# How the row-shifted copies of the value tile are made, in the input projection of a hybrid decoder layer

## The chip, the cores and the metric

One core of one Trainium2 chip runs the whole layer. The metric is the device time of one execution in microseconds (us); the kernel before takes 1537.65 us, the median of three runs that lie between 1537.08 and 1538.68.

## What is computed

The reference is one decoder layer over 256 rows of 2048 features, in float32, batch 1. Cut to what matters here:

```python
h = rmsnorm(x, norm_mix_w)
proj = h @ w_in                                   # q, k, v, z, b, a, pool, g_a, g_b
q, k, v, ... = split(proj)
qkv = silu(causal_dwconv(concat(q, k, v), conv_qkv_w))     # CONV_QKV = 4 taps
q = l2norm(q) * HEAD_DIM ** -0.5 ; k = l2norm(k)           # 16 heads of 128
o = gated_delta_rule(q, k, v, g_log, beta)        # 4 chunks of 64 rows
y_a = rmsnorm(o, gdn_norm_w) * silu(z)
y_b = (causal_multiscale_pool(p_in) @ pool_w) * pool_scale
x = x + (sigmoid(g_a) * y_a + sigmoid(g_b) * y_b) @ w_out
x = x + (gelu(causal_dwconv(gate) + b) * up) @ w_down      # ffn, then a last rmsnorm
```

The depthwise convolution takes, for each feature, row i times tap 3, plus row i-1 times tap 2, row i-2 times tap 1 and row i-3 times tap 0; rows above the first are zero. A kernel that holds rows on partitions must therefore bring rows i-1, i-2 and i-3 to the partition of row i.

## The kernel before

Every large product is made from float32 weights that are split in two halves of fewer bits. A weight tile of 512 KB (128 partitions by 2 by 512) arrives by SyncE's queue (SP) as `raw` (L223, four buffers). ScalarE (ACT) casts it to `whi` (L317), VectorE (DVE) subtracts `raw - whi` to give `wlo` (L328), and TensorE (PE) does twelve 128x512 matmuls on each tile: L365 (`whi` with the high half of the rows), L366 (`whi` with the low half) and L367 (`wlo` with the high half), four of each. `gemm_a` runs eight such tiles for one 256x512 block of the projection. Up to two tiles beyond the current one are asked for ahead (AHEAD = 2); `whi` and `wlo` have three buffers. SP's instructions run in order, so a `raw` load that waits for its buffer, or any other transfer that waits, holds all transfers behind it.

The mixing stage, up to about 770 us, loops over g = 0..3 (four heads each). For each g it makes the blocks K, Q, V, P (pool), the gates and Z. A finished block is taken out of PSUM by `evict`: ACT scales it into the tile `ev` (L781, tag `ev`, a single buffer).

- K and Q are turned so that features lie on partitions, and convolved by `conv_silu`: ACT makes tap 3, DVE adds the three others as twelve instructions of about 254 columns (L839), ACT takes the tanh (L844), and DVE writes `kq` (L846). The working tile has tag `cy`, two buffers. Later DVE takes sums of squares of the heads (L906, from PE's small products at L901).
- V keeps its rows on partitions. `ev` is written by SP to the DRAM scratch `vrow` (L1122), behind three rows of zeros that ACT's queue has put there at the start (L774, from the tile `zr` that DVE clears at L771). Then `v_moved` multiplies `ev` by tap 3 into `vt` (DVE, L802) and reads three copies `mv` back from `vrow`, shifted by j = 1, 2, 3 rows (SP, L807). Copies 1 and 2 are in the two `cy` buffers, which they share with `conv_silu`; copy 3 has the buffer of tag `mv`. `v_conv` does for j = 1, 2, 3: `mv *= tap` (L816) and `vt += mv` (L817), then a tanh on ACT and one more product (L822).
- `gdn` then goes on with the heads: decays, `ga` (L920), small tables sent out to DRAM as `cdd` (L939) and brought back to many partitions as `lb`, the triangular inverse (L965, L967), and the state recurrence.

What stands where on each engine is decided at build time by a scheduler that places instructions by its own estimate of when they are ready, apart from places that `issue_after` ties to an earlier instruction (in `v_conv`, each tap follows a certain `wlo`). So the conv's instructions, the `wlo` subtractions and the sums of squares stand mixed on DVE in one fixed order, and the transfers of the conv and of the weights in one fixed order on SP.

Of the kernel before, what the change touches and what calls it, by code (L numbers as in the profile page):

```python
# [8 lines left out]
F32 = mybir.dt.float32  # L9
# [5 lines left out]
P = 128  # L15
S = 256
# [19 lines left out]
def kernel(  # L36
# [20 lines left out]
    nc = tc.nc  # L57
# [5 lines left out]
    dpool = ctx.enter_context(tc.tile_pool(name="dram", bufs=2, space=bass.MemoryType.DRAM))  # L63
# [5 lines left out]
    def nm(s):  # L69
        cnt[0] += 1  # L70
        return f"{s}_{cnt[0]}"
# [282 lines left out]
    def gemm_a(lh, ll, nk, steps=None, ps=None):  # L354

        ps = pm() if ps is None else ps
        for c in range(nk // 2) if steps is None else steps:
            if c == 1:
                while later:
                    later.pop(0)()  # L360
            hi, lo = weights()
            for kk in range(2):
                k = 2 * c + kk
                for t in range(2):
                    mm(ps[:, t, :], lh(k, t), hi[:, kk, :], start=(k == 0), stop=False)  # L365
                    mm(ps[:, t, :], ll(k, t), hi[:, kk, :], start=False, stop=False)  # L366
                    mm(ps[:, t, :], lh(k, t), lo[:, kk, :], start=False, stop=(k == nk - 1))  # L367
                side()
        return ps
# [65 lines left out]
    mp = mix.__enter__()  # L435
# [46 lines left out]
    def parts_x(pts):  # L482
        for k, pt in pts:
            high, low = (both(xhl, k)[:, n, :] for n in range(2))
            hi = nc.scalar.activation(high, pt, AF.Copy, scale=nmw[:, k : k + 1])
            lo = nc.vector.scalar_tensor_tensor(low, pt, nmw[:, k : k + 1], high.bitcast(F32),
                                                op0=ALU.mult, op1=ALU.subtract)
        return hi.ins, lo.ins
# [28 lines left out]
    with tc.manual_schedule(engines={mybir.EngineType.PE, mybir.EngineType.DVE, mybir.EngineType.Activation}):  # L517
# [21 lines left out]
        for c in range(4):  # L539
            if c:  # L540
                tile_k0(2 * c)
            if c < 3:
# [3 lines left out]
                last_act, last_dve = parts_x(pts[2:])  # L546
# [219 lines left out]


    SH = 3
    vrow = dpool.tile([4, SH + S, 512], F32, tag="vrow", bufs=1, name="vrow")
    zr = mp.tile([P, 2, 512], F32, tag="mv", name="zr")  # L770
    nc.vector.memset(zr[:SH, 0, :], 0.0)  # L771
    for g in range(4):
        with tc.issue_after(last_act):
            nc.scalar.dma_start(vrow[g, 0:SH, :], zr[:SH, 0, :])  # L774

    def evict(ps, by=None):

        by = rs1 if by is None else by
        e = mp.tile([P, 2, 512], F32, tag="ev", bufs=1, name=nm("ev"))
        for t in range(2):  # L780
            nc.scalar.activation(e[:, t, :], ps[:, t, :], AF.Copy, scale=by[:, t : t + 1])  # L781
        return e
# [17 lines left out]
    def v_moved(e, g, vt):  # L800

        nc.vector.tensor_tensor(vt, e, taps_of[g][3], op=ALU.mult)  # L802
        moved_of[g] = []
        splits_of[g] = len(splits)
        for j in (1, 2, 3):
            m = mp.tile([P, 2, 512], F32, name=nm("mv"), **(dict(tag="cy", bufs=2) if j < 3 else dict(tag="mv")))
            nc.sync.dma_start(m, vrow[g, SH - j : SH - j + S, :].rearrange("(t p) d -> p t d", p=P))  # L807
            moved_of[g].append(m)

    def v_conv(g, vt):  # L810
# [284 lines left out]
    for g in range(4):  # L1095
        kq = mp.tile([P, 4, 2, S], F32, tag="kq", bufs=1, name=nm("kq"))
        for kind, dst in ((1, kq[:, :, 0, :]), (0, kq[:, :, 1, :])):
            ps = ps_k0 if kind == 1 and g == 0 else gemm_a(xh, xl, KD)
            e = evict(ps)
# [19 lines left out]

            later.append(after_k)  # L1120
        e = evict(gemm_a(xh, xl, KD), rsh)
        nc.sync.dma_start(vrow[g, SH : SH + S, :].rearrange("(t p) d -> p t d", p=P), e)  # L1122
        later.append(lambda e=e, g=g, vt2=vt2: v_moved(e, g, vt2))


# [3 lines left out]
        e = evict(ps) if g == 3 else evict(ps, rsh)  # L1129
# [608 lines left out]
```

## Time and profile before

| what | value |
|---|---|
| median of three runs | 1537.65 us |
| the profiled execution's own time | 1538.56 us |
| its span in the profile | 1536.8 us |
| granted TensorE clock, mean | 0.998 |
| TensorE matmul busy | 1524.3 us, 99% of the span |
| VectorE busy | 1268.3 us, 83% |
| ScalarE busy | 853.1 us, 56% |
| GpSimd busy | 80.9 us, 5% |
| SyncE's queue, share of 16 DMA engines | 59.2% |

A row of a group names the line of the kernel, the engine, the operation, then what is written and what is read, the shape, and the time of it; in a timeline the start comes first, and a bracket at the end of a row tells how long the engine had been idle and what ended that. A matmul of 128x512 shows as 0.39 us though the next one starts 0.227 us after it, because matmuls overlap: a stall of TensorE shows as idle time only where it is longer than that overlap of 0.16 us. A row of waits tells who waited, for whom, how long in all, how many times, and the longest.

### The profile page before, as it was taken

Reading aid. Unit: us, or ns where it says so; the run is one execution under the profiler, and the core shown is the slowest. Engines: PE = TensorE matmul, PEld = TensorE weight load, DVE = VectorE, ACT = ScalarE, POOL = GpSimd, SP = SyncE. Lnnn points to the kernel's source line nnn. Section 1 sums busy time; section 2 is a strip of 40 time slices with the busy share of each in tenths; the row PEclk is TensorE's granted clock in tenths of the full one; section 3 lists DMA queues with packets and bytes.
Section 4 is the critical chain, followed back from the end, with each engine's and each line's share of the span. In section 5 each row is a group of like instructions: output and inputs, shape, how many; then the busy total and the mean of one; then the engine's idle time right before and its main releaser. Section 6 shows DMA issues by size and latency. Waiting matters only on the chain. (4 is left out here: it accounts for less than half of the span.)

```text
span 1536.8 us, 20233 instructions
## 1 busy us (share of the span) xinstructions
PE 1524.3 (99%) x7290; PEld 1255.4 (82%) x7290; DVE 1268.3 (83%) x1793; ACT 853.1 (56%) x1070; POOL 80.9 (5%) x105
## 2 busy tenths in 40 slices
PE   9999999999999999999999999999999999999997
PEld 8887888787878888788888888788888888888876
DVE  6788859896589858887567899999999886889896
ACT  6455446454455445454455666666666665555553
POOL 1010002000100000000000000000000011010200
PEclk9999999999999999999999999999999999999999
DMA  8776757776576766776588556656457478566662
GB/s 276 209 229 198 203 165 207 218 216 185 148 250 201 208 169 194 231 195 186 171 263 305 179 178 219 219 206 206 154 165 243 127 238 266 172 223 207 235 201 98
DMA packets 166515, 313.62 MB, mean 204 GB/s; under 512 B 19554, under 2 KB 23426, under 8 KB 166286
## 3 DMA queue, kind: packets, MB, share of 16 engines
q1 hardware_dynamic: 157280, 283.17, 59.2%
q0 software_dynamic: 7344, 27.27, 5.5%
q10 hardware_dynamic: 1790, 1.89, 0.4%
q8 instruction: 57, 0.93, 0.3%
q14 instruction: 44, 0.36, 0.1%
HBM read 303.33 MB, written 8.95 MB: 203 GB/s over the span
## 5 line engine op out<-in xcount | busy, mean ns | idle before, releaser
L317 ACT CAST whi<-raw 128x1024 fp32r<-128x1024 f32 x420 | 441.2, 1052 | 427.1 <-PE psm L366 270.0
L328 DVE TENSOR_TENSOR wlo<-raw,whi 128x1024 fp32r<-128x1024 f32 x418 | 507.7, 1220 | 146.0 <-ACT whi L317 140.2
L317 ACT CAST whi<-quad 128x1024 fp32r<-128x1024 f32 x182 | 190.5, 1053 | 136.8 <-PE psg L1418 43.5
L328 DVE TENSOR_TENSOR wlo<-quad,whi 128x1024 fp32r<-128x1024 f32 x182 | 220.0, 1219 | 30.0 <-ACT whi L317 29.4
L367 PE MATMUL psm<-wlo,xhl 128*128 128x512 f32 x432 | 169.5, 393 | 1.3 <-DVE wlo L328 1.2
L365 PE MATMUL psm<-whi,xhl 128*128 128x512 f32 x432 | 169.0, 391 | 0.0
L366 PE MATMUL psm<-whi,xhl 128*128 128x512 f32 x432 | 168.6, 390 | 0.0
L1418 PE MATMUL psg<-whi,fhl 128*128 128x512 f32 x504 | 127.2, 390 | 0.0
L1418 PEld LDWEIGHTS psg<-whi,fhl 128*128 128x128 f32 x504 | 94.5, 188 | 19.6
L367 PEld LDWEIGHTS psm<-wlo,xhl 128*128 128x128 f32 x432 | 81.1, 188 | 18.8 <-DVE wlo L328 2.2
L366 PEld LDWEIGHTS psm<-whi,xhl 128*128 128x128 f32 x432 | 81.1, 188 | 16.8
L365 PEld LDWEIGHTS psm<-whi,xhl 128*128 128x128 f32 x432 | 81.1, 188 | 16.7
L244 DVE TENSOR_TENSOR quad<-quad,quad 128x1024 f32<-128x1024 f32 x72 | 87.6, 1216 | 0.0
L1418 PE MATMUL psg<-wlo,fhl 128*128 128x512 f32 x252 | 69.9, 389 | 0.0
L1418 PE MATMUL psg<-whi,ups 128*128 128x512 f32 x216 | 58.9, 394 | 0.0
L1418 PEld LDWEIGHTS psg<-wlo,fhl 128*128 128x128 f32 x252 | 47.3, 188 | 9.9
L1403 PE MATMUL psm<-whi,hhi 128*128 128x512 f32 (+1 forms) x140 | 54.5, 389 | 0.1
L1403 PE MATMUL psm<-whi,hlo 128*128 128x512 f32 (+1 forms) x140 | 54.1, 386 | 0.0
L1403 PE MATMUL psm<-wlo,hhi 128*128 128x512 f32 (+1 forms) x140 | 54.0, 387 | 0.0
L365 PE MATMUL psm<-whi,mhi 128*128 128x512 f32 x128 | 50.8, 397 | 0.0
L367 PE MATMUL psm<-wlo,mhi 128*128 128x512 f32 x128 | 50.0, 390 | 0.0
L366 PE MATMUL psm<-whi,mlo 128*128 128x512 f32 x128 | 49.9, 390 | 0.0
(435 smaller groups left out, 2953.7 us busy)
## 6 DMA issues: line engine op xcount, KB each, us to landing
raw<-in_w_in_dram SPq DMA_DIRECT2D x224, 512.0 KB, 4.3
raw<-in_w_up_dram SPq DMA_DIRECT2D x104, 512.0 KB, 4.8
quad<-in_w_up_dram SPq DMA_DIRECT2D x72, 512.0 KB, 5.0
raw<-in_w_down_dram SPq DMA_DIRECT2D x56, 512.0 KB, 5.1
raw<-in_w_out_dram SPq DMA_DIRECT2D x32, 512.0 KB, 4.2
quad<-in_w_down_dram POOLq DMA_DIRECT2D x32, 512.0 KB, 5.3
mv<-vrow SPq DMA_DIRECT2D x12, 512.0 KB, 4.8
taps<-in_conv_qkv_w_dram SPq DMA_DIRECT2D x16, 256.0 KB, 6.6
```

Of the source, the lines that this page charges most:

```text
L244: nc.vector.tensor_tensor(out_, plus_, minus_, op=ALU.subtract)
L317: last_cast[0] = nc.scalar.copy(hi, raw).ins
L328: last_split[0] = nc.vector.tensor_tensor(lo, raw, hi.bitcast(F32), op=ALU.subtract).ins
L365: mm(ps[:, t, :], lh(k, t), hi[:, kk, :], start=(k == 0), stop=False)
L366: mm(ps[:, t, :], ll(k, t), hi[:, kk, :], start=False, stop=False)
L367: mm(ps[:, t, :], lh(k, t), lo[:, kk, :], start=False, stop=(k == nk - 1))
L1403: mm(ps[:, cs], lhs(kk), part_[:, kk, cs], start=(first and kk == 0 and n == 0), stop=(last and kk == 1 and n == 2), skip_group_check=shared)
L1418: mm(ps, lhs(kk), w[n][:, kk], start=(first and n == 0 and kk == 0 and lhs is high), stop=False, skip_group_check=True)
```

## The change

The scratch `vrow`, the zeros `zr` and their four transfers go. For each shift j the copy is now made inside the chip: GpSimd (POOL) clears the first j rows of the first half of `mv` (L801 of the changed kernel), and SP issues three transfers from `ev` to `mv`: 112 partitions moved by j (L802), the remaining 16 - j partitions (L803), and the last j partitions of the first half to the first j partitions of the second half (L804). Copy 1 is now in the buffer of tag `mv`, and copies 2 and 3 are in the `cy` buffers. The convolution's own arithmetic is the same. Line numbers of the changed kernel are 6 lower at `evict`, 3 lower from the convolution to the eviction of V, and 4 lower behind it.

```diff
     SH = 3
-    vrow = dpool.tile([4, SH + S, 512], F32, tag="vrow", bufs=1, name="vrow")
-    zr = mp.tile([P, 2, 512], F32, tag="mv", name="zr")
-    nc.vector.memset(zr[:SH, 0, :], 0.0)
-    for g in range(4):
-        with tc.issue_after(last_act):
-            nc.scalar.dma_start(vrow[g, 0:SH, :], zr[:SH, 0, :])
...
         for j in (1, 2, 3):
-            m = mp.tile([P, 2, 512], F32, name=nm("mv"), **(dict(tag="cy", bufs=2) if j < 3 else dict(tag="mv")))
-            nc.sync.dma_start(m, vrow[g, SH - j : SH - j + S, :].rearrange("(t p) d -> p t d", p=P))
+            m = mp.tile([P, 2, 512], F32, name=nm("mv"), **(dict(tag="cy", bufs=2) if j > 1 else dict(tag="mv")))
+            nc.gpsimd.memset(m[0:j, 0, :], 0.0)
+            nc.sync.dma_start(m[j : 112 + j], e[:112])
+            nc.sync.dma_start(m[112 + j :], e[112 : P - j])
+            nc.sync.dma_start(m[0:j, 1, :], e[P - j :, 0, :])
             moved_of[g].append(m)
...
         e = evict(gemm_a(xh, xl, KD), rsh)
-        nc.sync.dma_start(vrow[g, SH : SH + S, :].rearrange("(t p) d -> p t d", p=P), e)
         later.append(lambda e=e, g=g, vt2=vt2: v_moved(e, g, vt2))
```

The scheduler places the instructions anew. All four groups and all engines differ only up to the end of the mixing stage; behind it the orders are the same. Three places follow.

SP, in group 2, from the eviction of V on: before, one write to `vrow`, one weight tile, and the three reads of 512 KB.

```order
L1122 DMA vrow<-ev_4083 128x2x512
L223 DMA raw_4172<-in_w_in_dram 128x2x512
L807 DMA mv_4112<-vrow 128x2x512
L807 DMA mv_4114<-vrow 128x2x512
L807 DMA mv_4116<-vrow 128x2x512
L223 DMA raw_4190<-in_w_in_dram 128x2x512
```

After, in the same place (`mv_4120`, `mv_4125`, `mv_4130` are the copies 1, 2 and 3):

```order
L804 DMA mv_4120<-ev_4092 1x16x32
L802 DMA mv_4120<-ev_4092 112x1024
L803 DMA mv_4120<-ev_4092 15x1024
L802 DMA mv_4125<-ev_4092 112x1024
L803 DMA mv_4125<-ev_4092 14x1024
L804 DMA mv_4125<-ev_4092 2x512
L223 DMA raw_4189<-in_w_in_dram 128x2x512
L223 DMA raw_4207<-in_w_in_dram 128x2x512
L223 DMA raw_4225<-in_w_in_dram 128x2x512
L802 DMA mv_4130<-ev_4092 112x1024
L803 DMA mv_4130<-ev_4092 13x1024
L804 DMA mv_4130<-ev_4092 3x512
```

Five transfers became twelve, the copies stand where the write to DRAM stood, and the third copy stands three weight tiles further back.

DVE, in group 2, before: the convolution of V, the `wlo` of the next weight tiles and the sums of squares (L906).

```order
L816 TENSOR_TENSOR mv_4112<-mv_4112,taps_3817 128x1024
L328 TENSOR_TENSOR wlo_4158<-raw_4154,whi_4156 128x1024
L817 TENSOR_TENSOR vt_3813<-vt_3813,mv_4112 128x1024
L816 TENSOR_TENSOR mv_4114<-mv_4114,taps_3814 128x1024
L906 ISA jk_3946,ssk_3883<-psg_3942,ident 128x128
...
L816 TENSOR_TENSOR mv_4116<-mv_4116,taps_3814 128x1024
L817 TENSOR_TENSOR vt_3813<-vt_3813,mv_4114 128x1024
L906 ISA jk_3946,ssk_3883<-psg_3944,ident 128x128
...
L328 TENSOR_TENSOR wlo_4176<-raw_4172,whi_4174 128x1024
L817 TENSOR_TENSOR vt_3813<-vt_3813,mv_4116 128x1024
```

After (L813 and L814 are the lines L816 and L817 of before, L843 is L846, L903 is L906):

```order
L813 TENSOR_TENSOR mv_4120<-mv_4120,taps_3826 128x1024
L328 TENSOR_TENSOR wlo_4157<-raw_4153,whi_4155 128x1024
L813 TENSOR_TENSOR mv_4125<-mv_4125,taps_3823 128x1024
L843 SCALAR_TENSOR_TENSOR kq_3481<-th_3875,cy_3858 128x4x256
L814 TENSOR_TENSOR vt_3822<-vt_3822,mv_4120 128x1024
L328 TENSOR_TENSOR wlo_4175<-raw_4171,whi_4173 128x1024
L328 TENSOR_TENSOR wlo_4193<-raw_4189,whi_4191 128x1024
L814 TENSOR_TENSOR vt_3822<-vt_3822,mv_4125 128x1024
L813 TENSOR_TENSOR mv_4130<-mv_4130,taps_3823 128x1024
L328 TENSOR_TENSOR wlo_4211<-raw_4207,whi_4209 128x1024
L903 ISA jk_3955,ssk_3892<-psg_3951,ident 128x128
...
L814 TENSOR_TENSOR vt_3822<-vt_3822,mv_4130 128x1024
```

Between the first product of the conv and its last sum there stood two `wlo`; there now stand four and the `kq` of Q, and the first sum of squares comes two `wlo` later.

DVE, in group 3, before: from the `wlo` ahead of the conv to the `wlo` in the middle of it.

```order
L802 TENSOR_TENSOR vt_5350<-ev_5620,taps_5354 128x1024
L846 SCALAR_TENSOR_TENSOR kq_5009<-th_5403,cy_5386 128x4x256
L328 TENSOR_TENSOR wlo_5659<-raw_5655,whi_5657 128x1024
L328 TENSOR_TENSOR wlo_5677<-raw_5673,whi_5675 128x1024
L816 TENSOR_TENSOR mv_5649<-mv_5649,taps_5354 128x1024
L328 TENSOR_TENSOR wlo_5695<-raw_5691,whi_5693 128x1024
L817 TENSOR_TENSOR vt_5350<-vt_5350,mv_5649 128x1024
```

After (L796 is the product with tap 3, L836 the taps of Q's own convolution):

```order
L796 TENSOR_TENSOR vt_5367<-ev_5637,taps_5371 128x1024
...
L328 TENSOR_TENSOR wlo_5684<-raw_5680,whi_5682 128x1024
L836 SCALAR_TENSOR_TENSOR cy_5403<-psg_5393,cqw,cy_5403 128x254
L813 TENSOR_TENSOR mv_5665<-mv_5665,taps_5371 128x1024
L836 SCALAR_TENSOR_TENSOR cy_5403<-psg_5398,cqw,cy_5403 128x254
L328 TENSOR_TENSOR wlo_5702<-raw_5698,whi_5700 128x1024
L813 TENSOR_TENSOR mv_5670<-mv_5670,taps_5368 128x1024
L836 SCALAR_TENSOR_TENSOR cy_5403<-psg_5393,cqw,cy_5403 128x253
L814 TENSOR_TENSOR vt_5367<-vt_5367,mv_5665 128x1024
L836 SCALAR_TENSOR_TENSOR cy_5403<-psg_5398,cqw,cy_5403 128x253
L328 TENSOR_TENSOR wlo_5720<-raw_5716,whi_5718 128x1024
```

Two `wlo` stood between tap 3 and the first product on a copy; one stands there now, and Q's own convolution, which was over before tap 3, now lies between the steps of V's.

## Prediction

> **What bounds the kernel now.** I read the page's busy line first, then what PE waits for, then the stretches of the mixing stage.
>
> ```profile
> span 1536.8 us, 20233 instructions
> PE 1524.3 (99%) x7290; PEld 1255.4 (82%) x7290; DVE 1268.3 (83%) x1793; ACT 853.1 (56%) x1070; POOL 80.9 (5%) x105
> PE psm L367 <- DVE wlo L328: 1.5, 2, 1.2
> DVE mv L816 <- DMA mv<-vrow: 11.2, 4, 4.5
> ACT whi L317 <- DVE mv L816: 4.3, 1, 4.3
> ```
>
> TensorE is busy 99% of the span, and the change touches none of its matmuls. So nothing is won but where PE stands still, and nothing is lost but where PE is made to stand still. DVE waits 11.2 us for the row-shifted copies, four times, which looks like the prize; but PE waits for DVE's `wlo` only 1.5 us. What carries over from DVE to PE is read from the stretches (us, then PE, PEld and DVE busy):
>
> ```profile
> 140.00:160.00 20.00, 19.69 (x85) 15.53 (x86) 19.36 (x36) 12.13 (x19) 0.00 (x0) 1.00 0.74 210
> 280.00:300.00 20.00, 19.86 (x84) 15.47 (x83) 19.46 (x37) 8.54 (x9) 2.76 (x2) 1.00 0.58 170
> 440.00:460.00 20.00, 19.75 (x84) 15.37 (x82) 14.95 (x19) 9.20 (x10) 0.00 (x0) 1.00 0.80 267
> 460.00:480.00 20.00, 19.05 (x85) 15.22 (x85) 19.43 (x41) 7.88 (x10) 3.09 (x2) 1.00 0.56 163
> ```
>
> These are the stretches near the four convolutions where PE falls short of 20: 0.31 + 0.14 + 0.25 + 0.95 = 1.65 us. Group 3 has none. In three of the four DVE is at 97%, so a delay there goes straight into `wlo`. The idle time hides 0.16 us of each stall (a matmul shows 0.39 us, the next starts 0.227 us after it), so I count from start to start. The largest stall, in group 2, with the DVE rows that make it:
>
> ```profile
> 452.43 1.23 DVE L816 TENSOR_TENSOR mv<-mv,taps 128x1024 f32<-128x1024 f32 x1 [4.48 <-DMA mv<-vrow]
> 459.67 1.22 DVE L328 TENSOR_TENSOR wlo<-raw,whi 128x1024 fp32r<-128x1024 f32 x1
> 459.36 0.39 PE L366 MATMUL psm<-whi,xhl 128*128 128x512 f32 x1
> 460.95 0.50 PE L367 MATMUL psm<-wlo,xhl 128*128 128x512 f32 x1 [1.20 <-DVE wlo L328]
> 461.28 0.39 PE L365 MATMUL psm<-whi,xhl 128*128 128x512 f32 x1
> ```
>
> DVE stood 4.48 us until 452.43, worked without a gap, and began the `wlo` that PE needed at 459.59 only at 459.67. PE lost 460.95 - 459.36 - 0.23 = 1.36 us, and the matmul after it came 0.10 us late (0.33 instead of 0.23): 1.46 us. Groups 0 and 1:
>
> ```profile
> 99.69 1.23 DVE L816 TENSOR_TENSOR mv<-mv,taps 128x1024 f32<-128x1024 f32 x1 [2.25 <-DMA mv<-vrow]
> 137.35 0.42 DVE L965 TENSOR_TENSOR tmp<-lb,tb 128x248 f32<-128x248 f32 x1 [3.08 <-DMA lb<-cdd]
> 139.86 0.50 PE L367 MATMUL psm<-wlo,xhl1a 128*128 128x512 f32 x1
> 140.20 0.40 PE L365 MATMUL psm<-whi,xhl1a 128*128 128x512 f32 x1
> 148.25 0.39 PE L366 MATMUL psm<-whi,xhl2b 128*128 128x512 f32 x1
> 148.95 0.50 PE L367 MATMUL psm<-wlo,xhl2b 128*128 128x512 f32 x1 [0.31 <-DVE wlo L328]
> 275.97 1.23 DVE L816 TENSOR_TENSOR mv<-mv,taps 128x1024 f32<-128x1024 f32 x1 [2.29 <-DMA mv<-vrow]
> 281.54 0.39 PE L366 MATMUL psm<-whi,xhl 128*128 128x512 f32 x1
> 282.07 0.50 PE L367 MATMUL psm<-wlo,xhl 128*128 128x512 f32 x1
> ```
>
> Group 0 loses 148.95 - 148.25 - 0.23 = 0.47 and 0.11 behind it, and 0.11 at each of three restarts from 140.20 (0.34 instead of 0.23): 0.9 us. Group 1 loses 0.30 + 0.1 = 0.4. In all **2.8 us** is within the change's reach.
>
> **The change, part by part.** The path to the first product now goes from `ev` to `mv` by one transfer, not two:
>
> ```profile
> 442.40 0.37 SPq L1122 DMA_DIRECT2D vrow<-ev  x1
> 448.50 1.39 SPq L807 DMA_DIRECT2D mv<-vrow  x3
> 620.97 0.37 SPq L1122 DMA_DIRECT2D vrow<-ev  x1
> 624.73 1.39 SPq L807 DMA_DIRECT2D mv<-vrow  x3
> mv<-vrow SPq DMA_DIRECT2D x12, 512.0 KB, 4.8
> vrow<-ev SPq DMA_DIRECT2D x4, 512.0 KB, 4.9
> whole<-y POOLq DMA_DIRECT2D x3, 512.0 KB, 3.8
> xtd<-xt POOLq DMA_DIRECT2D x4, 512.0 KB, 6.1
> TT<-tbd SPq DMA_DIRECT2D x16, 32.0 KB, 2.2
> x<-in_x_dram SPq DMA_DIRECT2D x3, 512.0 KB, 8.6
> raw<-in_w_in_dram SPq DMA_DIRECT2D x224, 512.0 KB, 4.3
> L317 ACT CAST whi<-raw 128x1024 fp32r<-128x1024 f32 x420 | 441.2, 1052 | 427.1 <-PE psm L366 270.0
> L328 DVE TENSOR_TENSOR wlo<-raw,whi 128x1024 fp32r<-128x1024 f32 x418 | 507.7, 1220 | 146.0 <-ACT whi L317 140.2
> ```
>
> The reads waited 6.1 us (group 2) and 3.8 us (group 3) for the write to land. That goes. No row shows a copy from SBUF to SBUF. Its bounds: not under the 2.2 us of a small transfer, not over the 8.6 us of the slowest 512 KB one; I take 4.3 to 4.8, as the reads of the same size by the same queue. The rests of 13 to 15 rows (up to 60 KB) and the single rows (2 to 6 KB) I bound by 2.2 and 4.8, so they land with the large piece issued just ahead. On SP three issues at 1.39 / 3 = 0.46 us replace one: nine instead of four, 2.3 us more per group, which pushes later `raw` tiles back by up to 2.8 us. Cover: `raw` loads run about four tiles ahead (4 x 2.72 = 10.9 us, against 4.3 for landing, 1.05 for `whi`, 1.22 for `wlo`); about 4 us remains, and beyond it each us would cost one.
>
> [...]
>
> The POOL clears cost at most the 0.77 us of POOL's mean instruction (80.9 / 105), on an engine busy 5%. Copies 2 and 3 are in `cy`, so the third clear waits for Q's `kq` to release its buffer; behind it on SP stand weight loads and on POOL small work for the heads, whose readers come after the convolution. In group 2 that puts the third copy's landing near 458, and DVE comes to its product about then. Removing the early clear and four small transfers changes nothing: at that time PE is fed by other work.
>
> Group by group, with copy 1 issued where the write was issued:
> - **Group 0.** Copy 1 lands about 93 to 94, before DVE asks at 97.4 (99.69 less 2.25). The 2.25 us go. DVE is then full to 134 and sends its decay table earlier by as much; the 3.08 us wait for `lb` shrinks to about 0.9 and the 0.9 us of PE stalls, which lie in a saturated stretch just behind it, should go. Gain 0.9 (nothing, if the table's own transfers set it).
> - **Group 1.** Copy 1 lands about 271 instead of 275.97. DVE's order changes, its work does not; the `wlo` in question ends 2 us before PE asks. Gain 0.4.
> - **Group 2.** Copy 1 lands at about 447.5, so 4.48 us of waiting shrink to little. In its place stand the later `kq` and the wait for copy 3; adding 1.14 us per 128x1024 step in the new order leaves each `wlo` 0.9 to 1.5 us ahead of PE. Gain 1.46.
> - **Group 3.** Here is no stall to win, and the new order is tighter:
>
> ```profile
> 620.98 1.23 DVE L802 TENSOR_TENSOR vt<-ev,taps 128x1024 f32<-128x1024 f32 x1
> 628.71 1.22 DVE L816 TENSOR_TENSOR mv<-mv,taps 128x1024 f32<-128x1024 f32 x1 [2.22 <-DMA mv<-vrow]
> 624.61 0.39 PE L367 MATMUL psm<-wlo,xhl1a 128*128 128x512 f32 x1
> ```
>
> PE begins the low half of a tile at 624.61; three tiles on, with the heads' small products now behind them, it needs `wlo` at 624.61 + 3 x 2.72 = 632.77. From copy 1's landing DVE does two conv products and a sum (3 x 1.14), three taps of Q (0.4 each) and two `wlo` (1.14 + 1.22) ahead of it: 6.9 us. So the landing may be 625.9 at the latest. Issued at 621.4, at 4.3 to 4.8 us it lands at 625.7 to 626.2: a stall of 0 to 0.3, and I charge 0.3.
>
> **The sum**: 2.8 - 0.3 = 2.5 us off the profiled execution's 1538.56: 1536.1. That execution was 0.9 above the median of the runs, so against the median 1537.65: **1535.2 us**, 0.16% less. This kernel's measurement tells about 0.2% (3.1 us) from no change, so most of this forecast lies within it.
>
> **The rivals.**
> - **Only the plain stalls go.** Group 0's chain over `lb` stays, or group 2's stall is replaced by one behind `kq` and copy 3. Then 0.4 + 1.46 - 0.3, or 0.9 + 0.4 - 0.3: 1536.1 to 1536.7. For it: the new DVE order holds four `wlo` and a `kq` in the same stretch. Still no measurable change.
> - **The copies land late, and the kernel is slower.** Place: group 3, where DVE's wait for copy 1 stands ahead of two `wlo`. The price is one us per us beyond 625.9. At 6.1 us (`xtd`) that is 1.6 there, and about half of group 2's and group 1's gain is lost: about 1538. At 8.6 us it is 4.1; groups 1 and 2 then get copy 1 at 276 and 451, as before, and gain nothing: 1537.65 + 4.1 - 0.5 = 1541. It decides from about 8 us. Against it: every 512 KB row by SP inside the kernel lies at 4 to 5 us.
> - **SP is blocked.** The third copy waits for `kq`, and `raw` loads stand behind it; if the 4 us cover is gone in one or two groups by 2 us each, the time is 1535.2 + 2 to 4, about 1538.
> - **More goes than I see.** DVE gains 11 us of slack in all, and if it also removes restarts of 0.1 to 0.2 us at other tiles (some ten), 1 us more: 1534.2.
> - **The change doesn't remove the wait**, because DVE's new place for the product comes as late as before: about 1537.7.
>
> **How the numbers follow.** Forecast (both groups of stalls gone, 1534.6 to 1536) 0.42; only the plain stalls 0.15; SP blocked, small delay or no effect 0.13; more than I see 0.16; slower by late copies 0.14. Faster by over 0.2% is under 1534.6: the fourth case and some of the spread of the first, 0.22. Slower is over 1540.7: 0.14. Within: 0.64. The range takes the first four cases and the late copies up to 8.6 us: 1533.9 to 1541.0.
>
> **What would show it.** Right: no wait of DVE for `mv` over 2 us in groups 0 to 2; copy 1 lands within 5 us of its issue; PE full at 460:480 but for a few tenths; PE's wait at `wlo` near 633 at most 0.3 us. Wrong: landing times over 6 us, PE idle in 620:660, ACT's `whi` waiting for `raw` behind the copies, or a new wait of DVE for the third copy's `mv` that ends later than 460.

## The result, and the profile after

The changed kernel takes 1541.9 us, the median of 14 runs (1539.79 to 1547.43); the kernel before, run beside it, 1537.53 (1534.92 to 1539.68). The ratio is 1.0031, 95% interval 1.0022 to 1.0039: **4.4 us slower**, where 2.5 us faster was forecast and 1533.9 to 1541.0 was the range.

The page of the changed kernel, and what its PE and DVE wait for (us in total, times, the longest):

```profile
span 1540.7 us, 20299 instructions
PE 1524.2 (99%) x7290; PEld 1254.7 (81%) x7290; DVE 1266.7 (82%) x1792; ACT 852.5 (55%) x1070; POOL 83.6 (5%) x117
PE psm L367 <- DVE wlo L328: 4.5, 5, 1.5
PE psg L1008 <- DVE T L984: 1.4, 2, 0.7
DVE mv L813 <- DMA mv<-ev: 9.7, 5, 4.0
DVE tmp L962 <- DMA lb<-cdd: 13.5, 4, 5.5
```

PE's work is the same; its wait for `wlo` went from 1.5 to 4.5 us, and a wait for `T` (the inverse that the heads of group 3 need) is new. DVE's wait for the shifted copies hardly fell, 11.2 to 9.7. Its wait for `lb`, the decay table that returns from DRAM, is 13.5 us; before it was 5.2 in total. The stretches (us, PE busy second):

```profile
280.00:300.00 20.00, 19.03 (x81) 14.77 (x80) 19.14 (x41) 8.60 (x10) 2.01 (x2) 1.00 0.60 164
460.00:480.00 20.00, 20.00 (x86) 15.90 (x85) 18.00 (x43) 9.11 (x10) 2.02 (x2) 1.00 0.57 162
480.00:500.00 20.00, 19.19 (x89) 15.57 (x88) 14.61 (x19) 10.31 (x15) 0.00 (x0) 1.00 0.68 183
660.00:680.00 20.00, 18.53 (x88) 14.95 (x86) 14.06 (x21) 8.52 (x11) 0.00 (x0) 1.00 0.69 188
680.00:700.00 20.00, 19.04 (x84) 15.44 (x84) 19.39 (x38) 10.22 (x17) 0.00 (x0) 1.00 0.77 206
720.00:740.00 20.00, 18.57 (x160) 14.60 (x160) 14.09 (x26) 8.29 (x13) 0.00 (x0) 1.00 0.51 161
```

The old stall of group 2 at 460 is gone, as forecast. Group 1's has grown, a new one stands near 497, and three stand in group 3, behind the convolution: 1.47 + 0.96 + 1.43 = 3.9 us, about the whole difference of the two spans (1540.7 against 1536.8); in groups 1 and 2 the visible idle time is 0.83 more, 1.20 less and 0.81 more, which nearly cancels. The chain that ends in these three stalls is seen on POOL, SP, DVE and PE. First the end of the sums of squares (`nk` on POOL follows the last of them) and the decay table of group 3 before:

```profile
649.55 1.01 POOL L911 TENSOR_TENSOR nk<-ssk,half 128x4 f32<-128x4 f32 x1 [7.25 <-DVE ssk L910]
652.66 3.65 SPq L939 DMA_DIRECT2D cdd<-ga  x8
657.56 1.74 SPq L942 DMA_DIRECT2D lb<-cdd  x4
```

and the same of the changed kernel, with what comes ahead of the sums and what DVE and PE do behind the table:

```profile
635.20 0.52 POOL L801 MEMSET mv<- 3x512 f32 x1 [14.24 <-DVE vt L814]
641.70 1.23 DVE L813 TENSOR_TENSOR mv<-mv,taps 128x1024 f32<-128x1024 f32 x1 [3.20 <-DMA mv<-ev]
654.93 1.01 POOL L908 TENSOR_TENSOR nk<-ssk,half 128x4 f32<-128x4 f32 x1 [7.14 <-DVE ssk L907]
658.05 3.66 SPq L936 DMA_DIRECT2D cdd<-ga  x8
664.52 1.73 SPq L939 DMA_DIRECT2D lb<-cdd  x4
671.79 0.42 DVE L962 TENSOR_TENSOR tmp<-lb,tb 128x248 f32<-128x248 f32 x1 [5.46 <-DMA lb<-cdd]
673.01 1.22 DVE L328 TENSOR_TENSOR wlo<-raw,whi 128x1024 fp32r<-128x1024 f32 x1
674.29 0.50 PE L367 MATMUL psm<-wlo,phi 128*128 128x512 f32 x1 [1.47 <-DVE wlo L328]
721.19 0.24 PE L1008 MATMUL psg<-T,ga 32*32 32x32 f32 x2 [0.74 <-DVE T L984]
722.12 0.69 PE L1008 MATMUL psg<-T,ga 32*32 32x32 f32 x30 [0.69 <-DVE T L984]
```

The clear for the third copy had to wait for the sum `vt` over the second (L814), so this copy is asked for only at 635.2, where before all three were asked for from 624.73 on. DVE stands 3.20 us for it with all sums of squares of the group behind. The sums end 5.4 us later, the table is asked for 7.0 us later, and DVE stands 5.46 us for it with a `wlo` queued behind: PE waits 1.47. DVE is then full (19.39 of 20) and PE loses 1 us more near 684. `T` is late too, and PE's next products for the heads stand at a place written by hand, so PE waits 1.43 there. The copies themselves:

```profile
266.12 0.57 SPq L802 DMA_DIRECT2D mv<-ev  x1
266.75 0.85 SPq L803 DMA_DIRECT2D mv<-ev  x1
274.07 1.23 DVE L813 TENSOR_TENSOR mv<-mv,taps 128x1024 f32<-128x1024 f32 x1 [4.04 <-DMA mv<-ev]
mv<-ev SPq DMA_DIRECT2D x12, 448.0 KB, 6.6
mv<-ev SPq DMA_DIRECT2D x4, 60.0 KB, 5.4
```

A 112-row copy lands 6.6 us after its issue in the median, a rest of 60 KB after 5.4. In group 1 copy 1's second piece, issued at 266.75, is there only at 274.07, 7.3 us on. SP spends 0.57 us on a large piece and 0.8 on a rest.

Two theories came out of this. **O, the order:** the scheduler, seeing other transfers, put the heads' work (`kq`, sums of squares, `ga`) later among the `wlo`, and the chain from the sums to `T` has no slack. **C, the copies:** they land late, and nine long issues per group hold SP and the weight tiles behind them.

### The profile page after: what moved, and what is told of

It is laid out like the page before. It is cut to its first block, busy times and chain, and to the rows that moved or that the text cites. A ratio compares the mean times of both kernels' runs of the same rounds, so it can differ in the third digit from the quotient of the medians.

```text
span 1540.7 us, 20299 instructions
## 1 busy us (share of the span) xinstructions
PE 1524.2 (99%) x7290; PEld 1254.7 (81%) x7290; DVE 1266.7 (82%) x1792; ACT 852.5 (55%) x1070; POOL 83.6 (5%) x117
```

## The experiments

All ratios are to the kernel before, run on the same chip.

| kernel | median us | ratio | 95% interval |
|---|---|---|---|
| changed | 1541.90 | 1.0031 | 1.0022 to 1.0039 |
| e1_flat | 1540.59 | 1.0017 | 1.0009 to 1.0026 |
| e2_pin | 1543.36 | 1.0032 | 1.0020 to 1.0044 |
| e3_pool | 1538.84 | 1.0005 | 0.9996 to 1.0013 |
| e4_oldbuf | 1540.43 | 1.0020 | 1.0011 to 1.0029 |
| e5_hop | 1539.48 | 1.0009 | 1.0000 to 1.0018 |
| e6_order | 1537.90 | 1.0000 | 0.9991 to 1.0009 |
| e7_late | 1537.10 | 0.9997 | 0.9989 to 1.0006 |
| e8_127 | 1626.37 | 1.0573 | 1.0554 to 1.0592 |
| e9_g3 | 1541.08 | 1.0029 | 1.0018 to 1.0041 |
| e10_slack | 1546.62 | 1.0065 | 1.0052 to 1.0079 |
| e11_both | 1536.11 | 0.9991 | 0.9982 to 0.9999 |
| e12_tags | 1537.83 | 1.0003 | 0.9995 to 1.0012 |
| e13_one | 1536.41 | 0.9995 | 0.9986 to 1.0004 |

**e1_flat: the changed order, cheap copies.**

```diff
-            nc.gpsimd.memset(m[0:j, 0, :], 0.0)
-            nc.sync.dma_start(m[j : 112 + j], e[:112])
-            nc.sync.dma_start(m[112 + j :], e[112 : P - j])
-            nc.sync.dma_start(m[0:j, 1, :], e[P - j :, 0, :])
+            nc.sync.dma_start(m, e)
```

> Leaves out the shift: each copy is one transfer of all 128 rows, unmoved, and no clear, so the convolution adds unshifted rows. DVE's order is the changed kernel's, SP issues three copies per group, not nine. Theory O (the order: Q's kq and the sums of squares stand three to four weight tiles later in groups 2 and 3, so the decay table lands late and DVE waits for it ahead of a wlo): PE still loses about 3 us near 670-690 and 1.5 near 721; +3 to +5 us on the kernel before. Theory C (the copies land late and SP is held by nine long issues): at most +1 us.

Measured: +3.1 us by the medians (1540.59 against 1537.52), 2.6 by the ratio. Its whole copies of 512 KB land in 4.1 us and SP issues three per group, yet most of the loss is there. So C carries at most the smaller part. DVE's longest wait for the table is 3.8 us here. It waits for the third copy of group 3 here too, 1.97 us instead of 3.20, and the sums end 1.5 us later than before, not 5.4.

**e2_pin: kq tied.** A weight tile's `wlo` of a given number is issued behind an instruction that stood ahead of it before:

```diff
+    PINS = {137: (4,), 141: (5,), 196: (6,), 199: (7,)}
...
             behind_conv = ExitStack()
+            for early in PINS.get(len(splits), ()):
+                behind_conv.enter_context(tc.issue_after(k_conv[early]))
```

> The changed kernel with all its nine transfers, but kq of K and Q in groups 2 and 3 is tied to the place among the wlo that it had before (the first sums of squares then follow by themselves). Theory O: the 4.9 us of group 3 go, group 1's 0.8 stays, group 2's old stall is gone: -0.5 to +0.8 us on the kernel before. Theory C: still +3.5 to +4.5.

Measured: +5.8 by the medians, ratio 1.0032, no better than the changed kernel. This spoke against O as I had put it. As built, only the first sums had followed; the second pair of heads still stood two `wlo` later than before (209 against 207 in group 3), SP issued `lb` at 659.69 instead of 657.56, and DVE waited 3.7 us for it. Its profiled run was the shortest of its five, so where its other runs lose was not seen.

**e3_pool: the small pieces on another queue.**

```diff
             nc.sync.dma_start(m[j : 112 + j], e[:112])
-            nc.sync.dma_start(m[112 + j :], e[112 : P - j])
-            nc.sync.dma_start(m[0:j, 1, :], e[P - j :, 0, :])
+            nc.gpsimd.dma_start(m[112 + j :], e[112 : P - j])
+            nc.gpsimd.dma_start(m[0:j, 1, :], e[P - j :, 0, :])
```

> The rests and single rows go by POOL's queue, the 112-row pieces stay on SP. As built, kq and the sums of squares stand as before the change. Theory O: -1 to +0.5 us on the kernel before. Theory C: SP's share (six of nine issues) goes, the late landing of the 112 rows stays: +1.5 to +3.

Measured: +1.3 us by the medians, +0.05% by the ratio, not told from no change, though the 112-row pieces land in 7.7 us and the last rests by POOL's queue in 7.9. Both the order and SP's load had changed here, so it parts the theories only in that late landing alone does not cost 4 us.

**e4_oldbuf: the buffers of before** (`j < 3` for `j > 1` in the choice of the tag).

> The changed kernel with the buffers of before: copies 1 and 2 in cy, copy 3 in mv. As built, group 3's order is nearly that of before, group 2's is that of the changed kernel. Theory O: group 3's 4.9 us go, the rest stays: -0.5 to +1 us on the kernel before. Theory C: +3.5 to +4.5, since transfers and queue are the same.

Measured: +2.9. Between the two. `lb` is asked for at 658.90 and PE still waits 1.1 us for `T`; behind that wait the granted clock fell to 0.50 (last section).

**e5_hop: the kernel before, with group 3's table late.** The converse: the DRAM path and the order of before, and one transfer more in the chain.

```diff
         lb = mp.tile([P, B0, B0], F32, tag="dec0", name=nm("lb"))
+        if g == 3:
+            far = dpool.tile([8, P, B0], F32, tag="far", bufs=1, name=nm("far"))
+            nc.sync.dma_start(far.rearrange("q p i -> (q p) i"), cdd.rearrange("q p i -> (q p) i"))
+            cdd = far
```

> The kernel before, DRAM path and buffers and all, with one thing added: in group 3 the decay table cdd is copied once more inside DRAM before it is brought back, so that lb lands some 4 to 6 us later. DVE's order as built is that of before through the sums of squares; lb's first product stands at the 215th wlo, as in the changed kernel. Theory O (group 3's chain of the heads has no slack, and its lateness is what costs): +2.5 to +5 us on the kernel before, with PE losing time near 670-690 and at L1011 near 720. Theory C (the copies themselves and SP's issues cost): no copy is changed, so -0.3 to +0.7.

Measured: +2.1 by the medians, ratio 1.0009 (1.0000 to 1.0018): slower, but less than 2.5. `lb` was issued at 660.44, 2.9 us later than before, not 4 to 6. In its trace `wlo` is never late in group 3, and all of the loss is at the hand-placed products:

```profile
656.20 0.57 SPq L943 DMA_DIRECT2D far<-cdd  x1
660.44 2.15 SPq L946 DMA_DIRECT2D lb<-far  x4
716.66 0.24 PE L1015 MATMUL psg<-T,ga 32*32 32x32 f32 x2 [1.13 <-DVE T L991]
717.59 0.69 PE L1015 MATMUL psg<-T,ga 32*32 32x32 f32 x30 [0.69 <-DVE T L991]
```

So the chain's end has no slack in the kernel before: about 3 us of lateness costs 1.8 us of waiting there, and some 1.2 us more behind it (last section).

**e6_order: nine transfers, order of before.** `PINS` now ties kq, each sum of squares and each `ga` of groups 1 to 3.

```diff
+    PINS = {79: [("kq", 1, 1)], 83: [("kq", 1, 0)], 85: [("sum", 1, 0)], 86: [("sum", 1, 1)],
+            92: [("sum", 1, 2), ("sum", 1, 3), ("ga", 1, 2), ("ga", 1, 3)],
...
+            behind_conv.enter_context(tc.issue_after(placed[early]))
```

> The changed kernel with all nine transfers per group on SP, and in groups 1 to 3 kq, every sum of squares and every ga tied to the place among the wlo that they had before. Theory O: group 3's loss goes: -1.5 to +1 us on the kernel before. Theory C: +3 to +4.5.

Measured: 1537.9, ratio 1.0000. The loss is gone with all nine transfers on SP and their long issues (0.55 to 0.86 us each in group 3); DVE still waits 4.5 us in all for the copies (9.7 in the changed kernel). C falls as a cause by itself. Within the changed order the late landing may still add to the loss: e1, with that order and quicker copies, loses less than the changed kernel.

**e7_late: the kernel before, conv products held back.**

```diff
-            with tc.issue_after(splits[splits_of[g] + n + (3 if g == 0 else 0)]):
+            with tc.issue_after(splits[splits_of[g] + n + (3 if g == 0 else 4)]):
```

> The kernel before, with the DRAM path, and the three products of V's convolution in groups 1 to 3 held back by four weight tiles, so that no wlo is queued behind a product that waits for its copy. As built the sums of squares then stand the same or up to four wlo earlier. Theory O: DVE's waits for mv and the stalls of 1.46 and 0.4 us go, group 0's 0.9 stays: -1 to -2.5 us on the kernel before. Theory C has nothing to say of it: 0 to -2.

Measured: 0.3 us less, interval on both sides of 1; a miss. In its profiled run the four stalls that I had counted are gone, but there is a new one: at 472 to 474 a `wlo` stands behind a held-back product, a sum and six `ga`, and PE loses 1.02 us.

```profile
460.00:480.00 20.00, 18.98 (x88) 15.56 (x87) 19.68 (x30) 10.01 (x14) 1.01 (x1) 1.00 0.47 129
```

So e7 doesn't show what the kernel gains without stalls. What the counted ones are worth is seen in e5's trace, whose program is that of before up to group 3's table:

```profile
140.00:160.00 20.00, 20.00 (x90) 16.57 (x89) 19.35 (x36) 12.45 (x19) 0.00 (x0) 1.00 0.75 222
280.00:300.00 20.00, 19.58 (x83) 15.20 (x82) 19.46 (x38) 8.54 (x9) 2.09 (x2) 1.00 0.58 164
440.00:460.00 20.00, 19.80 (x84) 15.45 (x83) 15.85 (x19) 8.84 (x10) 0.00 (x0) 1.00 0.76 261
460.00:480.00 20.00, 20.00 (x91) 15.95 (x90) 18.78 (x41) 9.40 (x11) 3.10 (x2) 1.00 0.61 168
```

The same instructions lose 0 + 0.42 + 0.20 + 0 = 0.62 us there, against 1.65 in the profiled run of before. So these stalls differ from run to run, and the profiled run of before was one of its longer ones. That the landing of transfers makes the difference is likely, but not shown.

**e8_127: without the 112-row piece.**

```diff
-            nc.sync.dma_start(m[j : 112 + j], e[:112])
-            nc.sync.dma_start(m[112 + j :], e[112 : P - j])
+            nc.sync.dma_start(m[j:], e[: P - j])
```

> The changed kernel with the 112-row piece and its rest as one transfer of 128 - j rows: 127, 126 and 125. DVE's order as built is that of the changed kernel. [...]

Measured: +89 us, two runs, where the changed kernel stands at +4.4.

```profile
88.01 9.53 SPq L802 DMA_DIRECT2D mv<-ev  x2
117.99 1.23 DVE L328 TENSOR_TENSOR wlo<-raw,whi 128x1024 fp32r<-128x1024 f32 x1 [22.36 <-ACT whi L317]
119.14 1.22 DVE L812 TENSOR_TENSOR mv<-mv,taps 128x1024 f32<-128x1024 f32 x1
92.00:94.00 2.00, 2.00 (x11) 1.65 (x10) 1.95 (x3) 1.82 (x2) 0.00 (x0) 1.00 0.06 25
```

The two large copies hold SP for 9.5 us, a `whi` waits 22.7 us for its weights, and in group 0 the first product starts at 119.14 instead of 99.69. From 92 to 94, while SP stands at these copies, the mean busy share of the 16 DMA engines is 0.06, at 25 GB/s (the last two numbers of the last row); in the same stretch of the changed kernel it is 0.84, at 241 GB/s. Whole copies of 128 unmoved rows by the same queue land in 4.1 us (e1); what makes the copies of this run so slow was not shown.

**e9_g3: ties of e6 in group 3 alone.** (`PINS` keeps only entries of group 3.)

> The changed kernel, with kq, sums of squares and ga tied to their places of before in group 3 alone; groups 1 and 2 keep the changed order. Theory O in its narrow form (only group 3's lateness costs, since only there PE's next products for the heads stand at a place fixed by hand): -0.5 to +1 us on the kernel before. If the order costs in all groups: +1.5 to +3.

Measured: +3.9: the narrow form of O falls. Its profiled run was the longest of its six. There group 3's own `kq`, tied to its old place, comes late (628.32, before 622.12), and `wlo` waits behind it. This suggests that lateness is handed on from group 2 to group 3. It is not shown alone, for DVE also waits 1.48 us for the third copy there, at 637.96, and `lb` is asked for as late as in the changed kernel (664.32).

**e10_slack: room at the hand-written place.**

```diff
         if g == 3:
-            yield
-            yield
+            for _ in range(8):
+                yield
```

> The changed kernel, its order on DVE and SP through the sums as it is, but in group 3 the products with T (L1008) are written three weight tiles later in PE's hand-made order: 8 us more room for the chain. Theory O: the wait of PE at L1008 (1.7 us with what follows) goes, the wlo stalls of 2.9 us near 674 and 684 stay: 1 to 2.5 us less than the changed kernel, unless the later products delay the merge behind them. Theory C: the changed kernel's time within 0.7.

Measured: +9.4, 4.7 more than the changed kernel: a miss. PE's wait at L1008 is gone, but the chain runs on to the end of the mixing stage, and PE stands there instead:

```profile
673.06 0.79 PE L367 MATMUL psm<-wlo,phi 128*128 128x512 f32 x1 [2.31 <-DVE wlo L328]
766.13 0.33 PE L410 MATMUL psg<-ident,sz 128*128 128x128 f32 x1 [2.70 <-DVE sz L1211]
767.18 1.12 PE L410 MATMUL psg<-ident,sz 128*128 128x128 f32 x7 [0.72 <-DVE sz L1211]
```

**e11_both: e6 with the products held back by three tiles** (the edit of e7 with 3 for 4).

> Copies inside the chip, the order of the heads tied as before, and the conv's products in groups 1 to 3 held back by three weight tiles. It joins the two edits that took stalls away in their profiled runs. If their gains add: -1.5 to -2.5 us on the kernel before. If they only remove stalls that other runs of the kernel before don't have either: within 1 us of it.

Measured: 1536.11, ratio 0.9991 (0.9982 to 0.9999): 1.1 us less than before by the medians. The gains don't add to 2; what is left is at the edge of what can be measured.

**e12_tags: the kernel before with the new buffers** (`j > 1` for `j < 3`).

> The kernel before, DRAM path and all, with only the buffers exchanged: copy 1 in mv, copies 2 and 3 in cy. As built the order on DVE, SP and PE is that of before. Both theories: within 0.7 us of the kernel before; anything else would be a cost of the buffers.

Measured: +0.03%. The exchange of buffers alone costs nothing that can be measured.

**e13_one: one tie.** The order as built differs in group 1's convolution already, but the `ga` of the first pair of heads still start as before (286.80 against 286.61). Behind them a single `wlo` slipped ahead of the six `ga` of the second pair, which start at 298.32 instead of 295.80. DVE of the changed kernel, and behind it of this one:

```
L910 TENSOR_TENSOR sj_2352<-sj_2352,beta 128x2x2
L328 TENSOR_TENSOR wlo_2790<-raw_2786,whi_2788 128x1024
L917 SCALAR_TENSOR_TENSOR ga_387_2348<-psg_2469,sj_2352,dec_392_2353 128x2x128
...
L917 TENSOR_TENSOR sj_2352<-sj_2352,beta 128x2x2
L924 SCALAR_TENSOR_TENSOR ga_387_2348<-psg_2469,sj_2352,dec_392_2353 128x2x128
...
L333 TENSOR_TENSOR wlo_2790<-raw_2786,whi_2788 128x1024
```

```diff
+    PINS = {92: [("ga", 1, 2), ("ga", 1, 3)]}
```

> The changed kernel with one tie alone: the wlo that had slipped ahead of the six ga instructions of group 1's second pair of heads stands behind them again, as before the change. As built, that single tie gives back the old places of kq, the sums of squares, ga and lb in groups 2 and 3 too; all nine transfers per group stay on SP. If the whole loss is the order that follows from that one step: within 1 us of the kernel before. If tying more by hand was needed: +2 us or more.

Measured: 1536.41, ratio 0.9995 (0.9986 to 1.0004). One tie takes back the whole loss. Its trace:

```profile
DVE mv L818 <- DMA mv<-ev: 6.4, 3, 3.8
DVE tmp L969 <- DMA lb<-cdd: 5.5, 3, 2.7
654.55 2.30 SPq L946 DMA_DIRECT2D lb<-cdd  x4
660.00:680.00 20.00, 20.00 (x90) 16.58 (x89) 16.92 (x30) 11.18 (x18) 0.00 (x0) 1.00 0.63 189
680.00:700.00 20.00, 20.00 (x90) 16.57 (x89) 18.74 (x42) 10.14 (x11) 0.00 (x0) 1.00 0.79 215
720.00:740.00 20.00, 20.00 (x147) 16.32 (x146) 13.41 (x21) 7.67 (x10) 0.00 (x0) 1.00 0.44 148
```

The wait for `lb` is back at 5.5 us (5.2 before). In group 3 the third copy is asked for at 624.71 and DVE does not wait for it, the table is asked for at 654.55, 10 us earlier than in the changed kernel, and PE is full where it stood. Group 1's stall is still there, at 0.70 us.

## Why the prediction was wrong

- **What bounds the kernel**: right. PE's own work is 1524.2 us against 1524.3, and all that moved is where it stood.
- **The prize of 2.8 us**: mis-sized. It was read from one execution. The same instructions lost 0.62 instead of 1.65 us of visible idle time in e5's run. No run shows 2.8 us; the most that any variant gained is e11's 1.1 us by the medians.
- **Groups 0 to 2**: in the changed kernel group 2's stall went, as said. Group 0's did not: PE is at 19.69 in 140 to 160, as before. DVE no longer waits for the copy there, but ACT's `whi` waits 3.3 us for a `raw` behind the copies, and DVE then 2.9 us for that `whi`. Group 1's did not either, it grew to 0.97 us. Copy 1 landed after 7.3 us, not 4.3 to 4.8, but its product still starts earlier than before (274.07 against 275.97); the stall grew because more stands between this product and the `wlo` that PE waits for, 7.45 us instead of 4.83 (to 281.52, before to 280.80): one `wlo` that stood ahead of the product before, one more `vt` and two more sums of squares. Landing was 6.6 us in the median and SP's issues mostly 0.57 to 0.85, not 0.46, so 6.2 us of SP per group where I had about 4. The bounds did not hold: one 112-row piece took 8.8 us (bound 8.6), and rests took up to 7.3 (bound 4.8). By e6 and e13 all this by itself costs nothing that can be measured.
- **The step that failed**: "adding 1.14 us per 128x1024 step in the new order leaves each `wlo` 0.9 to 1.5 us ahead of PE", and group 3's charge of 0.3. I priced the new order by the `wlo` within the convolution alone. I had shown that the sums of squares come two `wlo` later in group 2, and did not follow them on to `nk`, `ga`, `cdd`, `lb` and `T`. That chain had no slack: in group 3 it came 7 us later at `lb` and cost 3.9 us of PE. I had weighed the wait for the third copy in group 2 alone; in group 3 it is 3.20 us, ahead of the first sum. The charge of 0.3 was for copy 1, whose product starts at 625.18, in time.
- **The rivals**: none named it. The signs did: landing times over 6 us came, and so did a new wait for the third copy, but no price was put on what stands behind it. "The copies land late" had the right sign and group, 1541, by the wrong mechanism: near 633, where I looked for its stall, PE is full in the changed kernel.

What was not settled: how much of the loss is the changed order alone and how much the late landing within it (e1 leaves 1 to 2 us for the latter), which link costs how much in other runs than the profiled ones (e2 and e4 fit neither case), and why the scheduler lets that one `wlo` slip. With the tie SP's order changes too, so e13 shows that the new order costs the 4 to 5 us, not that DVE's part of it does so alone; e5 shows the price of the chain's end by itself, 2 us.

## What to carry to other kernels

When an automatic scheduler places the instructions, a change of transfers is a change of order everywhere behind it: follow each moved instruction to the last consumer of its chain, not only to the engine that waits next. Where the order moved, look for the early places that differ and undo one alone: here one tie was worth 5 us, more than the copies. And a stall of a microsecond in one profiled run is not yet a prize; see first whether another run of the same program has it.

## What the runs showed of the hardware

After some short waits of PE its next matmuls ran at half speed. In e5, after 1.13 + 0.69 us of waiting, they start 0.43 us apart instead of 0.23, for six matmuls, and the granted clock in that stretch is 0.55 (the third number from the end of a row):

```profile
718.00:720.00 2.00, 2.00 (x21) 1.75 (x16) 1.79 (x6) 1.03 (x4) 0.00 (x0) 0.55 0.18 68
720.00:722.00 2.00, 2.00 (x7) 1.55 (x6) 0.00 (x0) 0.83 (x1) 0.00 (x0) 0.60 0.67 222
```

That adds some 1.2 us (six times 0.2) to a wait of 1.8. e10 shows the same behind its 2.31 us wait (0.50 in 674 to 676), and e4 behind waits of only 0.37 + 0.69 us for `T`:

```profile
720.00:722.00 2.00, 2.00 (x6) 1.51 (x6) 0.14 (x2) 1.16 (x2) 0.00 (x0) 0.50 0.62 198
```

Behind the changed kernel's 1.47 us at 674 and 0.74 + 0.69 at 722 the clock stayed at 1.00. So the length of the wait alone does not decide it, and what does was not found. In these three runs the waits ahead of the half speed were 1.1 to 2.3 us in all. Stalls are therefore not priced by their length alone. And a copy from SBUF to SBUF of 112 moved rows is no faster here than a read of 512 KB from DRAM (6.6 against 4.8 us to landing), while a whole unmoved 512 KB copy by the same queue lands in 4.1 (e1); whether the move, the pieces or the number of transfers in flight makes the difference was not parted.
